# A two-layer DiT on one core: gate sums on VectorE, shorter head norms, a new first-head order and reordered feed-forward openings

## Chip, core and metric

The program runs on 1 core of one Trainium2 chip. The metric is the device time of one execution in microseconds (us). A core has five engines with a queue of instructions each: TensorE (PE in the profile), VectorE (DVE), ScalarE (ACT), GpSimd (POOL) and SyncE (SP, which issues the DMAs).

## What is computed

Two transformer blocks over 512 image tokens and 256 context tokens with D = 1024; only the image rows are returned. Both blocks are modulated by `silu(c) @ ada_w + ada_b` (six chunks: shift, scale and gate for mixer and feed-forward), with one vector for image and one for context tokens. In short:

```
h = concat(image, context)
layer 0:  u = rms_norm(h) * (1 + scale) + shift
          q, k, v = u @ w_qkv;  q, k = rope(rms_norm_per_head(q)), rope(rms_norm_per_head(k))
          h += gate * (softmax(q k^T / 8) v @ w_o)          # 16 heads, 4 key heads of 64
          h += gate_f * swiglu(modulate(rms_norm(h)))       # hidden 2816
layer 1:  HGRN2: q, gate, z_fw, z_bw, v = u @ w_in; f = lb + (1 - lb) sigmoid(z)
          two scans, forward and backward, 8 heads of 128; h += gate * (o @ w_o)
          h += gate_f * swiglu(modulate(rms_norm(h)))
out = rms_norm(h[:512]) * w
```

The large products of float32 matrices are done as three products of fp32r halves.

## The kernel before

Everything lives in SBUF as [128 partitions, tokens], transposed so that channels are partitions. A float32 matrix is held as a high part and a low part: `split` (L86) lets ScalarE cast the high part (`whi`, `hnh`, ...) and VectorE or GpSimd subtract it for the low one (`wlo`, `hnl`, ...). `mm3` (L115 to L118) then issues three matmuls: high x high, high x low, low x high. The order of the instructions on each engine is set by the scheduler of the tile framework, from the program and its own costs; `pin` (keep_in_program_order) holds single instructions in the order written. PSUM has eight banks, given out by name from small pools; a bank comes free when its last reader is done.

The stages, with their places in the trace of before:

- Start (0 to 77 us). The modulation's columns are made in groups on TensorE (`ada_mm`, L185: four matmuls a step, with the two vectors as 32-column weights `cpad`), turned by `ada_put` (L187: a ScalarE copy into `arows`, a transpose into a bank `pta`, an addition on VectorE). `kv_group` (L447) modulates a 128-channel block `xhT[k]` with VectorE, splits it into `hnh` and `hnl`, multiplies it with the key and value weights, and steps the generator `gfill`, which does the remaining groups and then chunk 2, the attention's gate (`ada_chunk(2, ...)`: eight blocks of 128x1024, one step each).
- Query stage (77 to 184). Four weight groups g, each in two parts (`wq`), times three pairs of token tiles: a `q` bank gets 48 products of 128x256. `qk_norm_rope` (L515) squares on ScalarE (L521), sums with VectorE (`ss`, L524), takes the root on ScalarE (L526), does one Newton step with four small VectorE operations (L528 to L531), multiplies (`qhat`, L533; this frees the bank), and turns by the rope tables with VectorE and GpSimd (`qsin`). `k_first` does the same for the keys, casts them twice (`kd`) and transposes them in three `ptk` banks, of which ScalarE and VectorE copy halves to `kT`. `q_first` casts `qd`; GpSimd subtracts its low part; three blocks later eight `ptq` transposes follow. `dfill` does chunk 3 in between, with its sums in `apsum`.
- Attention (184 to 430): `sc` products, softmax on ScalarE and VectorE, `pt` transposes, `po`. Beside it, tiles of the residual are transposed (`rx`) and the gate matrices of chunks 4 and 5 multiplied (`pa`).
- The last part of the output projection with ffn0's opening (430 to 505, `start_attention`), ffn0 (to 977). In ffn openings, operands are block sums and differences of x (`blocks`), made by GpSimd and VectorE, and weights come by `split_next` (weight differences and their split).
- `first_head` (977 to 1003): the first head's three projections, q (image tokens only), z_fw and z_bw, while the last rows of the modulated input (`hn`) still come. Each of two reciprocal roots, image and context, goes: squares added to `acc_n`, `ssq` matmuls, `rc`, a diagonal `dg` on VectorE, `rstd` matmuls.
- Recurrence (1003 to 1436), then `hgrn_wo_last` with ffn1's opening (`start_recurrence`, to 1475): `hwo` products of the last two heads, residual (L687), a square on ScalarE and its addition to `acc_n` on GpSimd (L276), the root for each half of 256 tokens, x by VectorE and ScalarE, cast to `xw`, first `ffi` matmuls. `plain_split` makes the weights' parts.
- ffn1 (to 1813) and the output.

## Time and profile before

| | |
|---|---|
| time, median of 3 runs | 1823.32 us (1820.36 to 1823.44) |
| the profiled execution | 1821.68 us, its span 1819.9 us |
| TensorE busy | 1755.3 us, 96% |
| VectorE busy | 1300.5 us, 71% |
| ScalarE busy | 867.2 us, 48% |
| GpSimd busy | 637.7 us, 35% |
| mean granted TensorE clock | 0.990 |

The profile is one execution. A row of a group gives source line, engine, operation, output and inputs, count and durations. A wait is put down to the instruction whose end came last. The granted clock (PEclk) is 1.00 at full speed and 0.50 when TensorE is throttled. Time in which an engine is idle counts only where TensorE, or the end, waits for it.

### The profile page before, as it was taken

The page shows a single profiled execution, that of the slowest core. Times are in us where ns is not written, and L with a number is a line of the kernel's source. Part 1 is how long each engine was busy: PE and PEld are TensorE (multiplying, and loading weights), DVE is VectorE, ACT ScalarE, POOL GpSimd, SP SyncE. Part 2 cuts the span into 40 slices and gives each one's busy share as a digit, 9 for nine tenths or more (in the row PEclk, how much of TensorE's full clock was granted, in tenths as well). Part 3 has the DMA queues.
Part 4 walks back from the last instruction along what each step waited for, and adds up shares of the span by engine and source line. Part 5 has one row for each costly group of instructions (what it writes and reads, how often), then busy time and mean ns, then how long its engine had stood idle before and what let it go on. Part 6 is the DMA issues. An engine that isn't in the chain of part 4 may idle for free.

```text
span 1819.9 us, 30696 instructions
## 1 busy us (share of the span) xinstructions
PE 1755.3 (96%) x11749; PEld 1606.9 (88%) x11749; DVE 1300.5 (71%) x2291; ACT 867.2 (48%) x1768; POOL 637.7 (35%) x583
## 2 busy tenths in 40 slices
PE   8988999999999999999999999999999899999998
PEld 6778678988899999999998999899898799999997
DVE  4587588888888878787865555665747758786764
ACT  4342787676642424333354443343434445554545
POOL 1244254345522304131414333144325544443420
PEclk9999999999999999999999999999999999999999
DMA  8533520002124243445331211222211223333322
GB/s 319 176 105 84 163 79 24 1 24 64 30 87 129 73 137 93 146 133 153 108 116 34 70 59 59 70 82 70 81 56 38 67 59 112 101 106 106 99 60 83
DMA packets 213459, 166.45 MB, mean 91 GB/s; under 512 B 7952, under 2 KB 190400, under 8 KB 213312
## 3 DMA queue, kind: packets, MB, share of 16 engines
q1 hardware_dynamic: 213024, 163.43, 29.2%
...
## 4 chain that ended last, share of the span: by engine, by line
PE 78%; DVE 9%; POOL 4%; ACT 4%; issue 2%; DMA 2%; SPq 0%; POOLq 0%; DVEq 0%; ACTq 0%
PE ffo L118 5%; PE ffo L116 5%; PE ffo L117 5%; PE x L116 4%; PE x L117 4%; PE x L118 4%; PE pt L714 3%; PE y L118 2%; PE y L116 2%; PE y L117 2%; PE lv L1643 2%; PE hz L116 2%; PE hz L117 2%; PE hz L118 2%; PE sc L656 2%
## 5 line engine op out<-in xcount | busy, mean ns | idle before, releaser
L1650 POOL TENSOR_TENSOR KD<-KD,tot 128x384 f32<-128x384 f32 x96 | 102.6, 1092 | 82.1 <-ACT kc L1633 78.4
L704 POOL TENSOR_SCALAR pf<-pf,st 128x768 f32<-128x768 f32 (+1 forms) x96 | 73.6, 769 | 128.1 <-DVE st L703 91.6
L687 DVE SCALAR_TENSOR_TENSOR hT<-ffo,modc,hT 128x512 f32<-128x512 f32 (+1 forms) x122 | 78.7, 649 | 48.2 <-PE ffo L118 48.2
L118 PE MATMUL ffo<-gh,wlo_w 128*128 128x512 f32 (+1 forms) x304 | 102.9, 339 | 0.0
L117 PE MATMUL ffo<-gl,whi_w 128*128 128x512 f32 (+1 forms) x304 | 102.4, 337 | 0.0
L116 PE MATMUL ffo<-gh,whi_w 128*128 128x512 f32 (+1 forms) x304 | 102.0, 338 | 0.0
L239 DVE SCALAR_TENSOR_TENSOR adacc<-adw,csil,adacc 128x512 f32<-128x512 f32 x98 | 84.5, 871 | 7.5 <-DMA adw<-in_ada_w_dram 7.4
L93 DVE TENSOR_TENSOR ptl<-pt,pth 128x384 fp32r<-128x384 f32 (+1 forms) x160 | 79.9, 524 | 12.4 <-ACT pth L88 11.2
L88 ACT CAST pth<-pt 128x384 fp32r<-128x384 f32 (+1 forms) x160 | 69.9, 461 | 34.3 <-PE pt L714 22.6
L700 DVE TENSOR_REDUCE st<-sc 128x1 f32<-128x768 f32 (+1 forms) x96 | 74.2, 773 | 15.3 <-PE sc L657 12.6
L702 ACT ACTIVATE pf<-sc,st 128x768 f32<-128x768 f32 (+1 forms) x96 | 73.4, 765 | 19.3 <-DVE st L700 18.4
L1650 DVE TENSOR_TENSOR QD<-QD,tot 128x256 f32<-128x256 f32 x96 | 52.0, 582 | 41.2 <-PE lv L1643 41.1
L1633 ACT COPY kc<-KD 128x256 f32<-128x256 f32 x112 | 43.4, 414 | 75.8 <-PE lv L1643 43.8
L714 PE MATMUL pt<-ident,pf 128*128 128x128 f32 x448 | 72.2, 275 | 5.2 <-DVE ptl L93 3.9
L116 PE MATMUL ffo<-gh,foh 128*128 128x512 f32 (+1 forms) x186 | 71.4, 384 | 0.0
L118 PE MATMUL ffo<-gh,fol 128*128 128x512 f32 (+1 forms) x186 | 70.8, 381 | 0.2 <-DVE fol L93 0.2
L117 PE MATMUL ffo<-gl,foh 128*128 128x512 f32 (+1 forms) x186 | 70.9, 381 | 0.0
L1709 POOL TENSOR_SCALAR oss<-oss 128x4 f32<-128x4 f32 (+1 forms) x9 | 4.7, 524 | 181.8 <-DVE oss L1708 181.7
L1643 PE MATMUL lv<-QD,kc 128*128 128x128 f32 x448 | 63.4, 286 | 4.5 <-DVE QD L1650 2.4
L1643 PEld LDWEIGHTS lv<-QD,kc 128*128 128x128 f32 x448 | 58.7, 192 | 8.8 <-ACT kc L1633 3.8
L714 PEld LDWEIGHTS pt<-ident,pf 128*128 128x128 f32 x448 | 51.2, 140 | 14.4 <-issue 6.4
L117 PEld LDWEIGHTS ffo<-gl,whi_w 128*128 128x128 f32 x304 | 57.4, 189 | 6.9
...
## 6 DMA issues: line engine op xcount, KB each, us to landing
...
```

The costliest lines, as they stand in the source:

```text
L93: m = (eng or DVE).tensor_tensor(lo, src, hi.bitcast(F32), op=ALU.subtract)
L116: PE.matmul(ps, ahi, bhi, start=first, stop=False, **kw)
L117: PE.matmul(ps, ahi, blo, start=False, stop=False, **kw)
L118: PE.matmul(ps, alo, bhi, start=False, stop=last, **kw)
L239: pin(DVE.scalar_tensor_tensor(a, raw, cc, a, op0=ALU.mult, op1=ALU.add))
L687: DVE.scalar_tensor_tensor(hT[o][:, a:e], ps, mcol(layer, ch, o, v), hT[o][:, a:e], op0=ALU.mult, op1=ALU.add)
L700: DVE.tensor_reduce(st3[:, 0:1], ps[:, :nk], op=ALU.max, axis=AX.X, negate=True)
L702: ACT.activation(pf, ps[:, :nk], AF.Exp, bias=st3[:, 0:1], accum_out=st3[:, 1:2])
L704: POOL.tensor_scalar(pf, pf, st3[:, 2:3], 1.0, op0=ALU.mult, op1=ALU.mult)
L714: PE.transpose(pt[:, i * P : (i + 1) * P], pf[:, (i0 + i) * P : (i0 + i + 1) * P], ident)
L1643: PE.matmul(ps[:, cs], kc[:, cs], mv, start=True, stop=True)
L1650: eng.tensor_tensor(view, view, f, op=ALU.mult)
```

## The change

The edits, in the order of the program:

1. Chunk 2. `ada_shared` replaces `ada_chunk` there: VectorE multiplies six of the eight blocks by the vectors' columns and adds them up in two tiles `asum`, one for each vector (12 operations of 128x1024). TensorE does the steps of blocks 6 and 7 as before, and one product for each sum with `pick`, a matrix that adds over the partitions. The blocks from k = 4 on are modulated together ahead of it, the last two on ScalarE.
2. `qk_norm_rope` folds mean and epsilon into the root's scale and bias and into one combined Newton step: four VectorE operations follow the sum instead of six. `wk` and `wq` are scaled to match.
3. The keys' two casts and the second copy to `kT` go from VectorE to ScalarE. The last q block is first copied to SBUF by VectorE. Chunk 3's transposes go to the second half of the bank that holds its sums.
4. `first_head`: image tokens of all three projections come first, then the contexts; the context's root one step later; one weight split on VectorE instead of GpSimd; in `fo_out` the context's squares of rows up to 4 are added by VectorE.
5. `start_attention`: two weight steps (`split_next`) stand earlier. `start_recurrence`: the squares go to two sums, even rows on GpSimd and odd rows on VectorE (into `x[7]`); four weight splits move; the second root is taken after them; rows 6 and 7 of the last output projection come together.

The core of the diff:

```diff
-    def ada_put(pa, rows, dst, bias, nch, nk):
+    def ada_put(pa, rows, dst, bias, nch, nk, pt=None):
...
-        pt = bank("pta")
+        pt = bank("pta") if pt is None else pt
...
     def ada_chunk(ch, pa, rows, load):
+        pt = None if pa is None else pa[:, 256:512]
...
-    gfill.add(ada_chunk(2, None, lambda: stp.tile(...), xx_tile))
+    def ada_shared(ch, nsum):
...
+            k = step - 1
+            if k >= nsum:
+                products(raws[k], cpad[:, k], k == nsum, False)
+            for v in range(2 if 0 <= k < nsum else 0):
+                cc = csil[:, v, k : k + 1]
+                if k == 0:
+                    pin(DVE.tensor_scalar(sums[v], raws[k], cc, None, op0=ALU.mult))
+                else:
+                    pin(DVE.scalar_tensor_tensor(sums[v], raws[k], cc, sums[v], op0=ALU.mult, op1=ALU.add))
+            yield
+        for v in range(2):
+            products(sums[v], pick[:, v], False, v == 1)
...
+    def first_modulate(k):
+        for v, a, e in SP2:
+            xs, sc, sh = xhT[k][:, a:e], a_c0[:, k, v : v + 1], mcol(0, 0, k, v)
+            if k < KT - 2:
+                DVE.tensor_scalar(xs, xs, sc, sh, op0=ALU.mult, op1=ALU.add)
+            else:
+                ACT.activation(xs, xs, AF.Identity, bias=sh, scale=sc)
+        split(hn_hi[k], hn_lo[k], xhT[k])
+
+    def last_modulates():
+        for k in range(KT // 2, KT):
+            first_modulate(k)
+        yield from ada_shared(2, ADA_SUMS)
...
-        if sc != 1.0:
-            POOL.tensor_scalar(w, w, sc, 1.0, op0=ALU.mult, op1=ALU.mult)
+        POOL.tensor_scalar(w, w, -0.5 * sc / HD, 1.0, op0=ALU.mult, op1=ALU.mult)
...
-        DVE.tensor_scalar(ss, ss, 1.0 / HD, EPS, op0=ALU.mult, op1=ALU.add)
-        ACT.activation(sr, ss, AF.Sqrt)
+        ACT.activation(sr, ss, AF.Sqrt, bias=epst, scale=1.0 / HD)
         DVE.reciprocal(sr, sr)
         DVE.tensor_tensor(sa, sr, sr, op=ALU.mult)
-        DVE.tensor_tensor(sa, sa, ss, op=ALU.mult)
-        DVE.tensor_scalar(sa, sa, -0.5, 1.5, op0=ALU.mult, op1=ALU.add)
-        DVE.tensor_tensor(ss, sr, sa, op=ALU.mult)
+        DVE.scalar_tensor_tensor(sa, ss, HD * EPS, sa, op0=ALU.add, op1=ALU.mult)
+        DVE.scalar_tensor_tensor(ss, sa, -3.0 * HD, sr, op0=ALU.add, op1=ALU.mult)
...
-            DVE.tensor_copy(kd[:, :, :, i]...
+            ACT.copy(kd[:, :, :, i]...
...
-                    DVE.tensor_copy(dst[HD:P], pg[rows])
+                    ACT.copy(dst[HD:P], pg[rows])
...
+        if g == KVH - 1 and tp == 2:
+            raw = qst.tile([P, 512], F32, tag="kraw", bufs=2, name="qraw")
+            DVE.tensor_copy(raw, ps)
+            ps = raw
...
-                sumsq_add(acc_n[:, a:e], ..., POOL if v else DVE,
+                sumsq_add(acc_n[:, a:e], ..., POOL if v and o > 4 else DVE,
...
-        order = [[(0, 0), (1, 0)], [(1, 1), (2, 0)], [(2, 1)]]
+        order = [[(0, 0), (1, 0)], [(2, 0)], [(1, 1)], [(2, 1)]]
...
-                if n_ == 0 and k in (2, 4):
+                if (n_, k) in ((0, 4), (1, 1)):
                     next(ctx)
...
             for i in range(4):
                 b11, b12, b21, b22 = blocks(i)
                 pin(POOL.tensor_tensor(b12, b22, b12, op=ALU.subtract))
+            split_next()
...
+            split_next()
             plain_hidden(0, 1, *ps0)
...
-            split_next()
-            split_next()
...
-                    sumsq_add(acc_n[:, hs], fp, hT[o][:, hs], o, i == 0, POOL, tag="sw", bufs=2, width=512)
-                    if h == 0 and i == 0:
-                        plain_split(0, 0, "l")
-                    if h == 0 and i == KT - 1:
-                        plain_split(0, 1, "l")
-                    if h == 1 and i == 1:
-                        plain_split(1, 0, "l")
+                    if i % 2:
+                        sumsq_add(halfsums(h)[1], fp, hT[o][:, hs], o, i == 1, DVE, ...)
+                    else:
+                        sumsq_add(halfsums(h)[0], fp, hT[o][:, hs], o, i == 0, POOL, tag="sw", bufs=2, width=512)
+                    if h == 0 and i < 2:
+                        plain_split(0, i, "l")
+                    if h == 1 and i == 0:
+                        plain_split(1, 0, "hl")
...
             plain_split(1, 1, "l")
+            rc[1] = rstd_cols(fp, halfsums(1), H, "rc1")
```

How the queues move at three places. First VectorE at the end of the start. Before, these rows stand there (`wlo_wkv` is the low part of the last key and value weights, `modc` the finished gate columns, `wlo_wq` the first query weights, `vv` the values' low part):

```order
L93 TENSOR_TENSOR hnl_101<-xhT_309,hnh_93 128x768
L93 TENSOR_TENSOR hnl_102<-xhT_318,hnh_94 128x768
L93 TENSOR_TENSOR wlo_wkv_572<-raw_wkv_570,whi_wkv_571 128x1024
L195 TENSOR_TENSOR modc_82<-pta,cols_80 128x16
L93 TENSOR_TENSOR wlo_wq_749<-raw_wq_747,whi_wq_748 128x1024
L93 TENSOR_TENSOR wlo_wq_755<-raw_wq_753,whi_wq_754 128x1024
L93 TENSOR_TENSOR vv<-kv_323,vv 128x8x64
```

After, from the sums' third block on:

```order
L460 SCALAR_TENSOR_TENSOR asum_516<-adw_552,csil,asum_516 128x1024
L460 SCALAR_TENSOR_TENSOR asum_517<-adw_552,csil,asum_517 128x1024
L94 TENSOR_TENSOR wlo_wkv_584<-raw_wkv_582,whi_wkv_583 128x1024
L460 SCALAR_TENSOR_TENSOR asum_516<-adw_578,csil,asum_516 128x1024
L460 SCALAR_TENSOR_TENSOR asum_517<-adw_578,csil,asum_517 128x1024
L460 SCALAR_TENSOR_TENSOR asum_516<-adw_600,csil,asum_516 128x1024
L460 SCALAR_TENSOR_TENSOR asum_517<-adw_600,csil,asum_517 128x1024
L460 SCALAR_TENSOR_TENSOR asum_516<-adw_610,csil,asum_516 128x1024
L460 SCALAR_TENSOR_TENSOR asum_517<-adw_610,csil,asum_517 128x1024
L94 TENSOR_TENSOR vv<-kv_327,vv 128x8x64
L94 TENSOR_TENSOR wlo_wq_752<-raw_wq_750,whi_wq_751 128x1024
L198 TENSOR_TENSOR modc_82<-pta,cols_80 128x16
```

The sums surround the last key weights' low part; the first query weights' low parts now stand behind the values.

Second TensorE at the end of the query stage (`ptq` transposes of queries, `sc` scores, `rx` residual transposes, `pa` the products of chunk 4). Before:

```order
L603 MATMUL ptq<-ident,qd 128x128 x16
L656 MATMUL sc<-kT,qT_705 128x512
L657 MATMUL sc<-kT,qT_705 128x512
L656 MATMUL sc<-kT,qT_705 128x256
L657 MATMUL sc<-kT,qT_705 128x256
L603 MATMUL ptq<-ident,qd 128x128 x8
L682 MATMUL rx_2040<-ident,hT_2004 128x128 x2
L603 MATMUL ptq<-ident,qd 128x128 x8
L682 MATMUL rx_2040<-ident,hT_2004 128x128 x4
L185 MATMUL pa<-adw_2120,cpad 32x256 x4
```

After:

```order
L660 MATMUL ptq<-ident,qd 128x128 x16
L713 MATMUL sc<-kT,qT_707 128x512
L714 MATMUL sc<-kT,qT_707 128x512
L713 MATMUL sc<-kT,qT_707 128x256
L714 MATMUL sc<-kT,qT_707 128x256
L660 MATMUL ptq<-ident,qd 128x128 x8
L739 MATMUL rx_2014<-ident,hT_1978 128x128 x6
L713 MATMUL sc<-kT,qT_707 128x512
L714 MATMUL sc<-kT,qT_707 128x512
L713 MATMUL sc<-kT,qT_707 128x256
L714 MATMUL sc<-kT,qT_707 128x256
L660 MATMUL ptq<-ident,qd 128x128 x8
```

The second group of scores and the whole first residual tile now stand ahead of the last eight query transposes.

Third GpSimd in ffn1's opening (`wlo_w`, `w01l` low parts of weights, `sq` a row's squares, `rc` the root). Before, from the last head's root on:

```order
L93 TENSOR_TENSOR wlo_w<-raw_('w', 0, 0)_14910,whi_w 128x1024
L276 TENSOR_TENSOR acc_n<-acc_n,sq_14932 128x256
L276 TENSOR_TENSOR acc_n<-acc_n,sq_14939 128x256
L276 TENSOR_TENSOR acc_n<-acc_n,sq_14946 128x256
L276 TENSOR_TENSOR acc_n<-acc_n,sq_14953 128x256
L276 TENSOR_TENSOR acc_n<-acc_n,sq_14960 128x256
L276 TENSOR_TENSOR acc_n<-acc_n,sq_14970 128x256
L276 TENSOR_TENSOR acc_n<-acc_n,sq_14980 128x256
L276 TENSOR_TENSOR acc_n<-acc_n,sq_15008 128x256
L291 TENSOR_TENSOR rc<-rc,mhalf 128x2
```

After:

```order
L94 TENSOR_TENSOR wlo_w<-raw_('w', 0, 0)_14884,whi_w 128x1024
L94 TENSOR_TENSOR w01l<-raw_('w', 0, 1)_14886,w01h 128x1024
L280 TENSOR_TENSOR acc_n<-acc_n,sq_14916 128x256
L280 TENSOR_TENSOR acc_n<-acc_n,sq_14930 128x256
L280 TENSOR_TENSOR acc_n<-acc_n,sq_14953 128x256
L298 TENSOR_TENSOR rc<-rc,mhalf 128x2
```

A second weight split stands ahead of the sums, and three sums are left ahead of the root.

More of the change, by code (lines that the diff above doesn't have):

```diff
@@ L112, in load_split, with mm3 @@
         return hi, lo
-    def mm3(ps, ahi, alo, bhi, blo, first, last, onto=False):
+    def mm3(ps, ahi, alo, bhi, blo, first, last, onto=False, hold=False):
         kw = dict(skip_group_check=True) if onto else {}
-        PE.matmul(ps, ahi, bhi, start=first, stop=False, **kw)
+        m = PE.matmul(ps, ahi, bhi, start=first, stop=False, **kw)
+        if hold:
+            pin(m)
         PE.matmul(ps, ahi, blo, start=False, stop=False, **kw)
@@ L423, with products @@
         gfill.add(ada_group(*g_))
-    gfill.add(ada_chunk(2, None, lambda: stp.tile([P, 256], F32, tag="arows", bufs=2, name="arows2"), xx_tile))
+    pick = stp.tile([P, 2, 32], F32, name="pick")
+    POOL.memset(pick, 0.0)
+    for v in range(2):
+        POOL.memset(pick[:, v, v : v + 1], 1.0)
+    def ada_shared(ch, nsum):
+        pa = bank("pa")[:, 0:256]
+        sums = [stp.tile([P, D], F32, name=f"asum{v}") for v in range(2)]
+        def products(m, col, start, stop):
+            m4 = m.rearrange("p (b j n) -> p b j n", b=2, j=4)
+            for j in range(4):
+                PE.matmul(pa[32 * j : 32 * (j + 1)], col, m4[:, :, j], start=start, stop=stop)
+        raws = []
+        for step in range(KT + 1):
+            if step < KT:
+                raws.append(xx_tile(f"adw{ch}{step}"))
+                dma(raws[-1], ada_w[0, step * P : (step + 1) * P, ch * D : (ch + 1) * D])
+            k = step - 1
[8 more added lines that the diff above has]
+            yield
+        for v in range(2):
+            products(sums[v], pick[:, v], False, v == 1)
+        rows = stp.tile([P, 256], F32, tag="arows", bufs=2, name="arows2")
+        ada_put(pa, rows, modc[0][:, ch : ch + 1], ada_bias(0, ch, 1), 1, KT)
+    def first_modulate(k):
[10 more added lines that the diff above has]
+        yield from ada_shared(2, ADA_SUMS)
+    gfill.add(last_modulates())
     gfill.step(4)
@@ L450, in kv_group @@
             k = k0 + j
-            for v, a, e in SP2:
-                DVE.tensor_scalar(xhT[k][:, a:e], xhT[k][:, a:e], a_c0[:, k, v : v + 1], mcol(0, 0, k, v),
-                                  op0=ALU.mult, op1=ALU.add)
-            split(hn_hi[k], hn_lo[k], xhT[k])
+            if k < KT // 2:
+                first_modulate(k)
             for t in range(NT):
@@ L566, in k_first @@
         for i in range(2):
-            DVE.tensor_copy(kd[:, :, :, i].rearrange("p t h d -> p (t h) d"), r.rearrange("p t h d -> p (t h) d"))
+            ACT.copy(kd[:, :, :, i].rearrange("p t h d -> p (t h) d"), r.rearrange("p t h d -> p (t h) d"))
         POOL.tensor_tensor(kl, r, kd[:, :, :, 0].bitcast(F32), op=ALU.subtract)
@@ L971, in plain @@
                 ps[h] = xbank("ffi")[:, 0:H]
-            mm3(ps[h], hi[:, c], lo[:, c], xh[:, k % 4], xl[:, k % 4], first, last)
+            mm3(ps[h], hi[:, c], lo[:, c], xh[:, k % 4], xl[:, k % 4], first, last, hold=first and hold)
         gh, gl = {}, {}
@@ L1065, in fo_out @@
             if p_ == len(parts) - 1:
-                sumsq_add(acc_n[:, a:e], late_pool[0], hT[o][:, a:e], o, o == 0, POOL if v else DVE,
+                sumsq_add(acc_n[:, a:e], late_pool[0], hT[o][:, a:e], o, o == 0, POOL if v and o > 4 else DVE,
                           tag=f"g{8 + (o + v) % 2}", bufs=1, width=n)
```

49 lines of the change are left out of this document (31 added, 18 removed).

## The prediction

> **What bounds the kernel now.** I read the page first, then TensorE's waits, then the granted clock around the longest of them. The page's span, TensorE's busy row and the chain that ended last:
>
> ```profile
> span 1819.9 us, 30696 instructions
> PE 1755.3 (96%) x11749; PEld 1606.9 (88%) x11749; DVE 1300.5 (71%) x2291; ACT 867.2 (48%) x1768; POOL 637.7 (35%) x583
> PE 78%; DVE 9%; POOL 4%; ACT 4%; issue 2%; DMA 2%; SPq 0%; POOLq 0%; DVEq 0%; ACTq 0%
> ```
>
> TensorE works in 96% of the span, and the diff takes only a few matmuls away. So the time can fall almost only by what TensorE waits for. Its waits by releaser (total us, times, longest):
>
> ```profile
> PE q L117 <- DVE wlo_wq L93: 3.7, 2, 2.4
> PE sc L656 <- DVE qhat L533: 3.5, 1, 3.5
> ...
> PE pta L193 <- ACT kT L582: 3.3, 1, 3.3
> PE ssq L282 <- POOL acc_n L276: 3.2, 1, 3.2
> PE rstd L301 <- DVE dg L297: 3.1, 2, 1.6
> ...
> PE y L118 <- DVE wlo_w L93: 2.3, 1, 2.3
> ...
> PE ffi L116 <- ACT xw L88: 1.8, 1, 1.8
> ...
> PE ptk L578 <- ACT qT L606: 1.5, 1, 1.5
> ...
> PE ptk L578 <- DVE kT L588: 0.8, 1, 0.8
> ...
> PE h L116 <- DVE hT L687: 0.7, 1, 0.7
> ```
>
> All ten lie in stages that the diff touches. Four of them are followed by a stretch at half clock (columns of the windows: stretch, length, busy time of PE, PEld, DVE, ACT, POOL, then the granted clock):
>
> ```profile
> 121.20:128.00 6.80, 6.06 (x29) 6.06 (x30) 5.55 (x13) 1.85 (x5) 3.36 (x5) 0.50 0.01 1
> 134.90:138.30 3.40, 2.78 (x23) 2.78 (x24) 3.30 (x7) 0.21 (x1) 1.73 (x1) 1.00 0.47 137
> 179.20:182.60 3.40, 3.40 (x14) 3.21 (x15) 2.68 (x4) 0.64 (x2) 0.00 (x0) 0.50 1.19 289
> 493.20:500.00 6.80, 6.01 (x18) 5.14 (x17) 6.22 (x13) 5.62 (x13) 1.17 (x1) 0.50 0.35 97
> 1449.00:1455.80 6.80, 4.69 (x21) 4.38 (x21) 5.65 (x15) 5.17 (x15) 5.46 (x8) 0.50 0.00 1
> ```
>
> The wait of 3.3 (pta) ends at 121.9, that of 3.5 (sc) at 179.2, that of 2.3 (y) at 491.9, that of 3.2 (ssq) at 1447.3: each stands at or just before a clock of 0.50. After the 2.4 us wait for wlo_wq, which ends at 135.5, the clock stays 1.00. At half clock TensorE does half the work, so the stretches at 121, 179 and 1449 cost at most 3.4, 1.7 and 3.4 us besides the waits.
>
> The profiled execution took 1821.68 us, 1.8 of them outside the span; the median of the runs is 1823.32. I sum against 1821.7.
>
> **1. The start: eight TensorE steps become four.** A step of the gate's chunk and the kv matmuls around it, then VectorE there:
>
> ```profile
> 58.62 0.39 PE L118 MATMUL kv<-whi_wkv,hnl 128*128 128x512 f32 x1
> 58.95 0.64 PE L185 MATMUL pa<-adw,cpad 128*32 128x256 f32 x8
> 59.52 0.50 PE L116 MATMUL kv<-whi_wkv,hnh 128*128 128x512 f32 x1
> 59.85 0.40 PE L117 MATMUL kv<-wlo_wkv,hnh 128*128 128x512 f32 x1
> 60.09 0.39 PE L118 MATMUL kv<-whi_wkv,hnl 128*128 128x512 f32 x1
> ...
> 56.47 1.23 DVE L93 TENSOR_TENSOR wlo_wkv<-raw_wkv,whi_wkv 128x1024 fp32r<-128x1024 f32 x1
> 70.75 0.17 DVE L195 TENSOR_TENSOR modc<-pta,cols 128x16 f32<-128x16 f32 x1 [13.06 <-PE pta L193]
> ```
>
> Undisturbed kv matmuls start 0.24 apart (59.85 to 60.09); from 58.62 to 59.85 there are two of them and a step, so a step costs 1.23 - 0.47 = 0.76, and four fewer save 3.0 us. VectorE gets 12 operations of 128x1024, by the row at 56.47 some 1.2 each: 14 us into the 13.06 it stood idle. But in the new order ScalarE modulates blocks 6 and 7 and casts hnh for 4 to 6 ahead of the weights' high part for k = 4, and VectorE does six sums before wlo_wkv of k = 6. TensorE, 3 us early at k = 4, then waits about 1.5 and 0.5 us for these. SyncE's issues of the rope tables and of raw_wq stand behind the last two blocks of the sums and move from about 54 to about 60; they are first used after 77. I take a gain of 1.0 (from -2.5, if the sums delay the first key chain, to +1.5).
>
> **2. The query stage: VectorE gets shorter, a bank goes.** The groups of the norm, of the keys' casts and copies (count: min/median/max ns):
>
> ```profile
> L525 DVE TENSOR_SCALAR ss<-ss x15: 164/570/792, 76.0 to 176.3; 128x8 f32<-128x8 f32 x15
> L567 DVE CAST kd<-qrot x6: 416/418/427, 82.4 to 113.8; 128x512 fp32r<-128x512 f32 x6
> L588 DVE CAST kT<-ptk x6: 684/690/695, 95.5 to 129.2; 64x512 fp32r<-64x512 f32 x6
> ```
>
> Two operations less per call save 15 x (0.57 + 0.16) = 11; kd and kT go to ScalarE and save 6 x 0.42 + 6 x 0.69 = 6.6: together 17.7 us of VectorE. TensorE loses 12.7 us there: 3.7 + 3.3 + 1.5 + 0.8 by the waits, 3.4 by the clock. The chunk's transposes now go to the bank of their own sums, whose copy was long done: the pta wait and its half clock, 6.7 us, go whole. The other 6.0 I do not count whole: TensorE will run 6.7 us ahead of before, and VectorE must follow; ScalarE now makes both copies of a key bank one after the other. I count 1.3 of them: 8.0 in all (4 if the waits at key banks stay, 11 if nearly everything goes).
>
> The L525 operation takes 0.57 at the median and 0.16 alone. One of them, and what ran on GpSimd:
>
> ```profile
> 175.73 1.26 POOL L597 TENSOR_TENSOR qd<-qrot,qd 128x512 fp32r<-128x512 f32 x1 [1.33 <-DVE qd L596]
> 176.28 0.74 DVE L525 TENSOR_SCALAR ss<-ss 128x8 f32<-128x8 f32 x1
> ```
>
> It ends at 177.02, when GpSimd's qd ends (176.99). The Trainium skill, page "SBUF — State Buffer", section "Who interferes with whom", says that VectorE operations with two SBUF inputs, too, are locked out while a GpSimd operation reads SBUF. By that rule part of the stall would move to the next product of `ss` rather than go: about 0.4 of the 0.74 a call, and the 11 us of saving would be nearer 7, still enough to cover the 6.0.
>
> **3. The end of the stage.** The sc wait ends at 179.2 with the last qhat, the norm's product, which frees the q bank. Now VectorE copies that bank to SBUF ahead of the norm: it has cast the block before at 175.7 (GpSimd's qd starts then), and a copy of that size (0.69, as kT) ends at 176.4, while TensorE has 16 transposes to do. What comes behind on ScalarE, from the rows of before:
>
> ```profile
> 184.37 0.81 ACT L683 COPY hT<-rx 128x768 f32<-128x768 f32 x1
> 185.19 1.28 ACT L702 ACT_TABLE_LOAD   x1
> 186.49 0.90 ACT L702 ACTIVATE pf<-sc,st 128x768 f32<-128x768 f32 x1
> ```
>
> Wait and half clock, 3.5 + 1.7, go but for 0.3. New in the list: the second sc waits for ScalarE's copy of the first residual tile (0.8), the next residual for the first softmax (1.28 + 0.90, less some 0.5 of TensorE's own work: 1.7). Gain 5.2 - 0.3 - 0.8 - 1.7 = 2.4 (0 if the new waits reach the old, 4.5 if they are hidden).
>
> **4. ffn0's opening.** GpSimd's sums stand ahead of the two weight splits on VectorE's side of the list; but VectorE still has a dozen operations before the split that y waits for (2.3 us). Gain 0 (-2 to +3); the cover is gone if GpSimd's four sums alternate with VectorE's.
>
> **5. The first head.** VectorE's diagonal and what GpSimd did:
>
> ```profile
> 970.19 1.53 POOL L276 TENSOR_TENSOR acc_n<-acc_n,sq 128x256 f32<-128x256 f32 x2
> 971.76 0.69 DVE L297 TENSOR_TENSOR dg<-ident,rc 128x512 f32<-128x512 f32 x1 [2.38 <-POOL acc_n L276]
> ```
>
> One weight split and the context's first sums move from GpSimd to VectorE, so dg no longer waits for acc_n (its buffer): the first rstd wait of 1.6 shrinks to about 0.65, the second, 1.5, goes since the root comes a step later, h's 0.7 loses 0.2. The context step follows sooner, though, and may wait 0.3 for its rows. 0.95 + 1.5 + 0.2 - 0.3 = 2.3 (0 to 3.5).
>
> **6. ffn1's opening.** GpSimd before, and the casts that ScalarE moves ahead:
>
> ```profile
> 1435.05 2.39 POOL L93 TENSOR_TENSOR wlo_w<-raw_('w', 0, 0)_14910,whi_w 128x1024 fp32r<-128x1024 f32 x1
> 1439.67 8.21 POOL L276 TENSOR_TENSOR acc_n<-acc_n,sq 128x256 f32<-128x256 f32 x8 [2.23 <-ACT sq L275]
> 1460.14 1.04 ACT L88 CAST whi_w<-raw_('w', 2, 1)_15109 128x1024 fp32r<-128x1024 f32 x1
> ```
>
> TensorE's wait there, in its own row:
>
> ```profile
> 1447.26 0.61 PE L282 MATMUL ssq<-ones,acc_n 128*128 128x2 f32 x4 [3.23 <-POOL acc_n L276]
> ```
>
> Lost here: 3.2 (ssq) + 3.4 (clock) + 1.8 (ffi) = 8.4. After: GpSimd does two splits of 2.39 from 1435.05 on, some half a microsecond between them for the second's high part, to about 1440.3, then three sums instead of eight, the last behind two of VectorE's, to about 1443.5. TensorE came to ssq at 1447.26 - 3.23 = 1444.0; ssq now stands 18 half-width matmuls of 0.12 sooner, at 1441.8: it waits 1.7. ScalarE casts both halves of slice 2 (1.04 each, the second only when hwo's weights are free) before the first row of x: TensorE waits some 2.4 at ffi. With 0.3 for four more ssq matmuls 4.4 stay: gain 4.0 (0 if either new wait brings half clock again, 7 if GpSimd is not held up).
>
> **Nothing** for the pinned first ffi matmul, the scaled `wk` (one small GpSimd operation, long before use) and the root's scale and bias, which ride in an instruction that is there already.
>
> **Sum:** 1.0 + 8.0 + 2.4 + 0 + 2.3 + 4.0 = 17.7; 1821.7 - 17.7 = 1804.0 us.
>
> **Rivals.** (a) *The half clock stays.* Even if the waits go, the stretches at 0.50 may come wherever a new wait of about 2 us stands (parts 3 and 6): 3.4 + 1.7 + 3.4 = 8.5 more, 1812.5. For it: y's wait of only 2.3 was followed by one. Against: the wait at 121.9 has no successor in the new list. The Trainium skill, page "TensorE: Matmul & The Clock Gate", section "HAM oscillation — how this bites in real kernels", gives idle gaps above about 3.4 us as the limit; by that the gaps of 3.2 and 3.3 would not be the cause, and this rival is what follows. Here the clock of 0.50 after them speaks against it. Chance 0.12.
>
> (b) *The key banks wait for ScalarE.* The pta wait ended with a ScalarE copy of kT; if the next transposes wait for ScalarE's doubled copies instead, part 2 gives nothing: 1812.0. Against: ScalarE is busy under half of the stage. Chance 0.14.
>
> (c) *Slower: the sums.* If each of the 12 sums is held up by one GpSimd operation (2.39 as at 1435), VectorE ends 28.7 us later, and TensorE, in order, stands before the products; with 2 us of slack 26.7 more, 1830.7. It turns the sign from (17.7 + 2) / 12 = 1.6 us per sum. Against it GpSimd's work there:
>
> ```profile
> 48.00:75.00 27.00, 27.00 (x157) 17.52 (x156) 12.22 (x20) 8.86 (x12) 3.96 (x11) 1.00 0.57 200
> ```
>
> Eleven operations and 3.96 us in all. Chance 0.05.
>
> (d) *The waits are only replaced by others of their length*: 1821.7. Chance 0.05.
>
> **How the numbers follow.** The forecast has 0.64. The parts' ends, taken as independent (root of the squares), give 7.7 above and 5.7 below 1804.0; (a) and (b) lie just outside, so the range goes to 1815, and down to 1797. A measurement of this kernel tells about 0.2%, 3.6 us, from no change. Faster: 0.64 + 0.12 + 0.14 = 0.90; same: (d), 0.05; slower: (c), 0.05.
>
> **What would show it.** Right: no wait at the chunk's transposes and no half clock near 121, 179 and 1449; sc's wait under 1 us; ssq's near 1.7; ffi's first near 2.4; the first q matmul about 1 us before 77.1. Wrong: TensorE waiting at the products of the sums or at wlo_wkv for more than 2 us; VectorE's 128x1024 sums above 1.6; waits on kT of more than 3 us; half clock in the ffn1 opening.

## The result, and the profile after

The changed kernel takes 1813.51 us (median of 6 runs, 1809.85 to 1814.73), the kernel before 1822.62 (6 runs, 1820.24 to 1823.44): a ratio of 0.995, 95% interval 0.9939 to 0.9962, or 9.1 us less. Beside later experiments, on another chip, it was 1814.40 against 1819.84: 0.9971 (0.9959 to 0.9984), 5.4 us less. The change is faster, since both intervals lie below 1, by a third to a half of the forecast 17.7 us.

The page after: TensorE works in 97% of the span.

```profile
span 1810.8 us, 30614 instructions
PE 1752.7 (97%) x11725; PEld 1607.7 (89%) x11725; DVE 1308.5 (72%) x2267; ACT 875.3 (48%) x1784; POOL 637.4 (35%) x576
```

VectorE is busier, not less (1300.5 before): its 12 sums of 128x1024 outweigh what the norm and the keys save. TensorE's waits after, by releaser (total us, times, longest), those that answer to the list of the prediction:

```profile
PE y L121 <- DVE wlo_w L94: 3.4, 1, 3.4
...
PE ptk L631 <- ACT qT L663: 2.5, 1, 2.5
...
PE ffi L120 <- DVE xw L94: 2.3, 1, 2.3
PE ffi L117 <- ACT xw L89: 2.2, 1, 2.2
...
PE ssq L288 <- POOL acc_n L280: 2.0, 1, 2.0
...
PE q L120 <- DVE wlo_wq L94: 1.2, 1, 1.2
PE rstd L308 <- DVE dg L304: 1.2, 1, 1.2
...
PE sc L713 <- ACT hT L740: 0.9, 1, 0.9
PE rx L739 <- ACT pf L759: 0.9, 1, 0.9
```

The waits at chunk 3's transposes (`pta`, 3.3) and for the last `qhat` (`sc`, 3.5) are gone. The row for `ffi` from VectorE's `xw` is new; no term of the prediction had it. The stretches at half clock after, from 99 to 1455 us (stretch, length, busy time of PE, PEld, DVE, ACT, POOL, then the granted clock):

```profile
99.70:106.50 6.80, 6.09 (x35) 4.50 (x36) 5.37 (x13) 4.18 (x10) 2.17 (x5) 0.50 0.61 173
482.00:488.80 6.80, 6.15 (x19) 5.33 (x18) 5.99 (x12) 5.08 (x12) 0.25 (x1) 0.50 0.26 77
775.50:778.90 3.40, 3.40 (x16) 3.40 (x15) 2.97 (x6) 1.14 (x2) 0.00 (x0) 0.51 0.64 207
1393.40:1396.80 3.40, 3.40 (x17) 3.22 (x16) 3.40 (x10) 0.89 (x2) 0.45 (x1) 0.51 0.23 68
1441.10:1444.50 3.40, 3.40 (x18) 3.40 (x18) 2.45 (x7) 3.40 (x11) 1.84 (x3) 0.51 0.00 0
1451.40:1454.80 3.40, 3.40 (x18) 3.40 (x18) 0.49 (x2) 0.38 (x1) 0.00 (x0) 0.50 0.51 151
```

The one near 179 is gone; the one at 121 is gone, but one at 99.7 came; ffn1's opening has two, of 3.4 each, instead of one of 6.8.

Where the time went, from the starts of TensorE's own rows (the second profile of the change is that of the later measurement):

| part: from, to | forecast gain | before, us | after, us | after, second profile |
|---|---|---|---|---|
| 1: start to the first `q` matmul | 1.0 | 77.1 | 74.8 | 75.8 |
| 2: to the last `q` matmul | 8.0 | 96.5 | 91.3 | 91.4 |
| 3: to the last `po` matmul | 2.4 | 252.9 | 249.6 | 249.5 |
| 4: first `z` to first `w` of ffn0 | 0 | 13.3 | 13.7 | 13.0 |
| 5: first `ffo` to last `h` | 2.3 | 467.6 | 465.4 | 464.0 |
| 6: last pair of `ho` to the last `rstd` group | 4.0 | 30.4 | 33.2 | 33.2 |

The two rows of part 6, of before and of after:

```profile
1432.18 0.39 PE L1700 MATMUL ho<-S,QD 128*128 128x128 f32 x2
...
1462.60 0.61 PE L301 MATMUL rstd<-c,ones 128*128 128x128 f32 x4
```

```profile
1419.98 0.39 PE L1767 MATMUL ho<-S,QD 128*128 128x128 f32 x2
...
1453.22 1.05 PE L308 MATMUL rstd<-c,ones 128*128 128x128 f32 x4
```

Part 6 was to gain 4.0 and loses 2.8: this one stage is 6.8 of the missing 8.6 us (17.7 forecast, 9.1 measured). Part 2 lacks 2.8 and part 4 0.4; parts 1 and 3 bring 2.2 more than forecast in the first profile.

### The profile page after: what moved, and what is told of

Its sections match the earlier page's. It is cut to its first block, busy times and chain, and to the rows that moved or that the text cites. A ratio compares the mean times of both kernels' runs of the same rounds, so it can differ in the third digit from the quotient of the medians.

```text
span 1810.8 us, 30614 instructions
## 1 busy us (share of the span) xinstructions
PE 1752.7 (97%) x11725; PEld 1607.7 (89%) x11725; DVE 1308.5 (72%) x2267; ACT 875.3 (48%) x1784; POOL 637.4 (35%) x576
## 4 chain that ended last, share of the span: by engine, by line
PE 79%; DVE 8%; issue 4%; ACT 4%; POOL 4%; DMA 1%; POOLq 0%; SPq 0%; DVEq 0%; ACTq 0%
PE ffo L121 5%; PE ffo L117 5%; PE ffo L120 5%; PE x L117 4%; PE x L120 4%; PE x L121 4%; PE lv L1710 3%; PE pt L771 3%; PE y L121 2%; PE y L117 2%; PE y L120 2%; PE hz L117 2%; PE hz L120 2%; PE hz L121 2%; PE sc L713 1%
## 5 line engine op out<-in xcount | busy, mean ns | idle before, releaser
L1717 POOL TENSOR_TENSOR KD<-KD,tot 128x384 f32<-128x384 f32 x96 | 102.5, 1091 | 81.8 <-ACT kc L1700 78.0
L120 PE MATMUL ffo<-gl,whi_w 128*128 128x512 f32 (+1 forms) x304 | 102.5, 337 | 0.0
L757 DVE TENSOR_REDUCE st<-sc 128x1 f32<-128x768 f32 (+1 forms) x96 | 74.0, 772 | 10.4 <-PE sc L714 9.0
L771 PEld LDWEIGHTS pt<-ident,pf 128*128 128x128 f32 x448 | 51.2, 140 | 13.8 <-issue 6.2
```

Of the source, the lines that this page charges most:

```text
L120: PE.matmul(ps, ahi, blo, start=False, stop=False, **kw)
L757: DVE.tensor_reduce(st3[:, 0:1], ps[:, :nk], op=ALU.max, axis=AX.X, negate=True)
L771: PE.transpose(pt[:, i * P : (i + 1) * P], pf[:, (i0 + i) * P : (i0 + i + 1) * P], ident)
L1717: eng.tensor_tensor(view, view, f, op=ALU.mult)
```

## Why part 6 loses: GpSimd's new split

VectorE and GpSimd of after, where TensorE waits for `xw`, each in its own timeline:

```profile
1443.14 0.41 DVE L94 TENSOR_TENSOR xw<-x,xw 128x256 fp32r<-128x256 f32 x1
...
1447.67 2.56 DVE L94 TENSOR_TENSOR xw<-x,xw 128x256 fp32r<-128x256 f32 x1
```

```profile
1447.42 2.53 POOL L94 TENSOR_TENSOR w11l<-raw_('w', 1, 1)_14890,w11h 128x1024 fp32r<-128x1024 f32 x1
```

and TensorE:

```profile
1450.29 0.38 PE L120 MATMUL ffi<-xw,whi_w 128*128 128x256 f32 x1 [2.27 <-DVE xw L94]
```

One line of the whole diff, not among those printed above, chooses the engine of these splits:

```diff
-            pool_ = (j, i) == (0, 0) or j > 1 and i if layer else j == 0
+            pool_ = j == 0 or i if layer else j == 0
```

The new rule gives the low part of weight (1, 1) to GpSimd, too. GpSimd's split starts 0.25 us ahead of VectorE's low part of x, and that operation, 0.41 us a little earlier, takes 2.56: it ends at 1450.23, 0.28 after GpSimd's. TensorE stands for 2.27. This is the rule that the prediction cited for the norm's products (the Trainium skill, page "SBUF — State Buffer", section "Who interferes with whom": a VectorE instruction with two inputs in SBUF is blocked, not slowed, while a GpSimd instruction reads SBUF). The trace agrees, and the price is larger here: 2.15 us on the one operation, where the prediction took about 0.4 for a call of the norm. The prediction's working had counted GpSimd's two splits of weight 0 and overlooked this third one.

Four kernels tested it. The kernel before took 1821.8 us beside experiments 1, 2, 3 and 8, 1821.24 beside 4 to 7, and 1819.84 beside 9 to 12; a ratio is to that time, with its 95% interval.

**Experiment 1: that split back on VectorE.**

```diff
-            pool_ = j == 0 or i if layer else j == 0
+            pool_ = j == 0 or j > 1 and i if layer else j == 0
```

> The changed kernel with one split, w11l of slice 1's second part, back on VectorE; nothing else moves. Theory A (GpSimd's split of 2.53 us locks VectorE's low part of x out, 2.56 us for an operation of 0.41, and so makes TensorE's wait of 2.27 at ffi and the half clock behind it): the wait falls below 0.5 us, the time from 1813.5 to between 1809.5 and 1811.5. Rival B (VectorE is late anyway, since the second root stands ahead of that low part, and now has 1.2 us more to do): the wait stays above 1.5 us and the time within 1 us of 1813.5.

Measured: 1812.13 us, ratio 0.9947 (0.9931 to 0.9963), not to be told from the change itself, and outside both theories' ranges of time. Its first `q` matmul came 2.6 us later in the profiled run, with a DMA wait of 2.2 that ended at 34.6 us in the start, so the stage must be read by itself. There the `ffi` wait for `xw` is gone, and so is the second half clock. VectorE's rows at that place:

```profile
1450.36 0.75 DVE L94 TENSOR_TENSOR xw<-x,xw 128x256 fp32r<-128x256 f32 x2
1451.03 1.21 DVE L94 TENSOR_TENSOR w11l<-raw_('w', 1, 1)_14890,w11h 128x1024 fp32r<-128x1024 f32 x1
```

Two operations on x in 0.75, then the split in 1.21, half of what it takes on GpSimd. From `ho` to `rstd` it is 30.6 us (33.2 with the change): 2.6 back, so the wait is theory A's, and with the half clock behind it it makes 2.6 of the 6.8 that the stage lacks.

**Experiment 2: the whole of part 6 undone**, all else as changed.

> The changed kernel without the whole edit of ffn1's opening (start_recurrence, rows 6 and 7 of the last output projection, the split rule and the held matmul as before). Theory A (the edit of ffn1's opening costs about 2 us in all, since a new wait and two half-clock stretches replace what it saves): 1810 to 1812.5, so faster than the changed kernel. Rival B (it saves the 4 us forecast, and the shortfall lies elsewhere): 1816.5 to 1818.5. Rival C (neither gain nor loss): 1812.5 to 1814.5.

Measured: 1810.61 us, 0.9945 (0.9931 to 0.9959); the stage takes 31.4 us, with the old wait of 3.2 at `ssq` and a half clock of 10.2 us. So part 6 as it was made costs 1.9 us in its stage (33.24 against 31.37), though the changed kernel had less half clock there, 6.8 us.

**Experiment 3: the split back, and ScalarE's casts of slice 2 after x.** The prediction had put TensorE's wait at the first `ffi` down to those two casts of 1.04. ScalarE in after, ahead of the first row of x:

```profile
1436.32 1.05 ACT L89 CAST whi_w<-raw_('w', 2, 0)_15074 128x1024 fp32r<-128x1024 f32 x1 [1.18 <-PE hwo L120]
...
1437.79 1.03 ACT L89 CAST whi_w<-raw_('w', 2, 1)_15076 128x1024 fp32r<-128x1024 f32 x1
1438.72 0.51 ACT L1019 ACTIVATE x<-x,modc 128x256 f32<-128x256 f32 x1
```

```diff
+            pool_ = j == 0 or j > 1 and i if layer else j == 0
...
-            plain_split(2, 0, "l")
+            plain_split(2, 0, "hl")
-            plain_split(2, 1, "l")
+            plain_split(2, 1, "hl")
```

> As e1_split_back, and the two casts of slice 2's high weights on ScalarE held behind the first rows of x. Theory A: TensorE's wait at the first ffi falls from 2.24 to about 1.2 us, and the lock-out wait goes: 1808 to 1810.5. Rival B (the first ffi waits for the root and the chain behind it, not for the casts): its wait stays above 2 us and the time is that of e1_split_back.

Measured: 1808.82 us, 0.994 (0.9923 to 0.9956). The first `ffi` wait is 1.5 (2.2), so the two casts make 0.8 of it (2.24 to 1.48) and not the whole; in what is left ScalarE itself waits 1.07 for VectorE's first row of x. The stage is 29.3 us: 3.9 under the change, 1.1 under before, and still 2.9 above the 26.4 that the forecast makes it (30.4 - 4.0). It has 3.4 us at half clock.

**Experiment 4: part 6 alone on the kernel before.**

> Kernel: the kernel before with the change's part at ffn1's opening alone. Theory A (as it was made, this part costs: GpSimd's second split holds VectorE's low part of x, and TensorE waits at the first products): slower by 1 to 3 us, 1823 to 1825 against 1821.8. The recorded forecast: 4.0 us faster, 1817.8. If half clocks decide it by chance: anywhere between, with a half clock between 1440 and 1456 in the profile or without.

Measured: 1826.40 us, 1.0038 (1.0025 to 1.005): slower, by 5.2 us, theory A's sign and more than its 1 to 3. The stage takes 35.9 us (30.4). Its waits there:

```profile
PE ssq L286 <- POOL acc_n L278: 3.0, 1, 3.0
PE ffi L116 <- ACT xw L88: 2.5, 1, 2.5
PE ffi L119 <- DVE xw L93: 2.3, 1, 2.3
```

The wait for `xw` is there to the tenth, so it belongs to part 6 and to nothing else in the change. That the part costs 5.5 us in its stage here, and 1.9 by experiment 2, lies only in part in the clock. This profile has 10.2 us at half clock in the stage, the changed kernel's 6.8; the opening as it was before has 6.8 in the kernel before (30.4 us) and 10.2 in experiments 2, 5 and 6 (31.4, 31.5, 31.1 us). At equal half clock the part costs 2.8 (33.2 against 30.4, with 6.8) and 4.5 to 4.9 (35.9 against these three, with 10.2). The first two waits here are 1.2 us longer in sum than in the changed kernel; the rest of the difference stays open. That the part costs time is shown; how much depends on what stands around it.

## Why part 2 gives 5.2: the end of VectorE's chain sets the stage

The prediction valued the query stage by TensorE's waits: 6.7 us for chunk 3's transposes and the half clock behind them, and 1.3 of the rest. The first edit can be made alone.

**Experiment 5: only the bank of chunk 3's transposes**, on the kernel before.

```diff
+        pt = None if pa is None else pa[:, 256:512]
...
+        pt = bank("pta") if pt is None else pt
```

> Kernel: the kernel before with one edit, the chunk's transposes in the bank of its own sums. It removes the wait of 3.3 us for ScalarE's kT and the half clock behind it, 6.7 us together by the recorded working. Theory A (VectorE's chain to wlo_wq sets the stage, and what TensorE gains ahead of it is handed back at the next wait for wlo_wq, which grows): 0 to 2 us faster, 1819.8 to 1821.8, with a wait for wlo_wq above 4 us. Theory B (the wait and its half clock are the loss, as the prediction counted): 6.7 us faster, 1815.1, waits for wlo_wq unchanged at 3.7.

Measured: 1822.01 us, 1.0004 (0.9995 to 1.0013): nothing. The 3.3 us are gone from its list of waits, and come back at `wlo_wq` (two waits of 2.4 and 1.3 before, one of 5.1 now) and at `whi_wq` (new); the wait for `qhat` stands as before:

```profile
PE q L117 <- DVE wlo_wq L93: 5.1, 1, 5.1
PE sc L657 <- DVE qhat L534: 3.5, 1, 3.5
PE q L116 <- ACT whi_wq L88: 1.6, 1, 1.6
```

What stands in the way is the low part of the third weight group's second half. The matmul that waits for it, with its wait, of before, of this kernel, and of the change:

```profile
135.52 0.39 PE L117 MATMUL q<-wlo_wq,hnh 128*128 128x256 f32 x1 [2.42 <-DVE wlo_wq L93]
```

```profile
134.77 0.58 PE L117 MATMUL q<-wlo_wq,hnh 128*128 128x256 f32 x1 [5.14 <-DVE wlo_wq L93]
```

```profile
129.59 0.39 PE L120 MATMUL q<-wlo_wq,hnh 128*128 128x256 f32 x1 [1.21 <-DVE wlo_wq L94]
```

Counted from each profile's first `q` matmul (77.08, 76.43, 74.77), it is released after 58.4, 58.3 and 54.8 us, whatever TensorE had lost on the way: if TensorE is early, it waits longer. Experiment 4 shows the same with its query stage left as it was before: there the `pta` wait was 1.85 and no half clock followed it, the wait for `wlo_wq` was 5.14, and the release came after 58.5 us (135.14 less 76.68). The weight arrives when VectorE's list says so. So only what shortens that list counts, and the change took 3.6 us out of it. The other 1.6 of the 5.2 lie behind the release (38.1 us to the last `q` matmul before, 36.5 after), where a second wait for `wlo_wq`, 1.3 at 156.6 us, is gone. The list of after, up to the split:

```profile
119.07 1.32 DVE L596 TENSOR_TENSOR qrot<-qhat,cwq 128x256 f32<-128x256 f32 x2
121.17 0.69 DVE L605 TENSOR_TENSOR qrot<-qrot,qsin 128x512 f32<-128x512 f32 x1 [0.78 <-POOL qsin L601]
...
123.36 0.20 DVE L581 RECIPROCAL ss<-ss 128x8 f32<-128x8 f32 x1 [0.29 <-ACT ss L580]
...
127.25 0.69 DVE L605 TENSOR_TENSOR qrot<-qrot,qsin 128x512 f32<-128x512 f32 x1 [1.20 <-POOL qsin L601]
...
128.32 1.22 DVE L94 TENSOR_TENSOR wlo_wq<-raw_wq,whi_wq 128x1024 fp32r<-128x1024 f32 x1
```

VectorE waits in it for GpSimd's `qsin` and ScalarE's root. The 17.7 us of VectorE's work that the prediction counted as saved (by chance the same number as its whole forecast) could not turn into as much time: it is saved over the whole stage, partly behind the release, and the list is a chain over three engines, in order on each. Little of the saving moved on to the products of `ss` behind it. In the third of the 15 calls the second product now stands while GpSimd reads, 1.30 instead of 0.17 (VectorE, then GpSimd):

```profile
90.84 1.30 DVE L583 SCALAR_TENSOR_TENSOR ss<-ss 128x8 f32<-128x8 f32 x1
```

```profile
90.81 1.31 POOL L654 TENSOR_TENSOR qd<-qrot,qd 128x512 fp32r<-128x512 f32 x1 [1.26 <-DVE ss L582]
```

It ends at 92.14, GpSimd's `qd` at 92.12, as the Trainium skill's rule in the section named above has it; but before the change the first product of the same call had taken 1.26. The other 14 calls have this product at 0.17. Over the stage the norm's products and scalings took 19.5 us before and 9.9 after: 9.6 of the 11 us counted were saved, not the 7 that the prediction expected by that rule (its 15 calls of 0.4 would even have left 5).

**Experiment 6: the query stage's part alone** (parts 2 and 3) on the kernel before.

> Kernel: the kernel before with the query stage's part of the change alone (the chunk's transposes in the bank of its sums, the shorter norm, the keys' casts and second copies on ScalarE, the copy of the last q bank ahead of its norm). Theory A (what the trace after shows: the stage itself gains 5.2 us, because the weights' low part stands at the end of a chain on VectorE that did not get shorter by as much as TensorE got earlier; the end of the stage gains 3.3): 8.5 us faster than before, about 1813.3 against 1821.8, with a wait for wlo_wq between 1 and 4 us left. The recorded forecast (8.0 + 2.4 = 10.4): 1811.4, with that wait gone. Theory C (the gain of the stage is given back later, by other phases of the clock): under 6 us, above 1815.8.

Measured: 1812.34 us, 0.9954 (0.9942 to 0.9965): 8.9 less, theory A's 8.5. The interval, 6.4 to 10.6 us, does not quite exclude the forecast's 10.4; the trace does: the query stage takes 91.1 us, and a wait of 3.5 for `wlo_wq` is left. This part alone brings as much as the whole change (9.1 and 5.4), so the other parts come to little in sum.

**Experiment 7: a shorter norm.** On the kernel of experiment 3, the correction step is left out of the norm, as its expectation says.

```diff
-        DVE.tensor_tensor(sa, sr, sr, op=ALU.mult)
-        DVE.scalar_tensor_tensor(sa, ss, HD * EPS, sa, op0=ALU.add, op1=ALU.mult)
-        DVE.scalar_tensor_tensor(ss, sa, -3.0 * HD, sr, op0=ALU.add, op1=ALU.mult)
```

> Kernel: the fastest one so far (the change with GpSimd's extra split back on VectorE and ScalarE's casts of slice 2 behind the first rows of x, 1808.8 us), in which the norm of the query stage leaves out the correction step, three operations of 128x8 on VectorE per call, 45 in all (a part of the computation that is left out; a scalar of the norm's weights is set to suit). Theory A (VectorE's chain to wlo_wq sets the query stage's length): three operations of 0.17 to 0.2, and up to 1.3 where one is held up by GpSimd, go from each of six calls ahead of the wait: the wait for wlo_wq of 2.5 shrinks to under 1, the stage from 92.2 to 89 or 90, the time is 2 to 3 us less, about 1806. Theory B (the stage is set by TensorE and ScalarE, and the wait for wlo_wq is only where it shows): no change, 1808.8, the stage stays within 0.5 of 92.

Measured: 1805.68 us, 0.9929 (0.9912 to 0.9945), 3.1 under the kernel of experiment 3 by the medians of two chips, 2 by the ratios, whose intervals overlap. The stage shows it better. Waits of its query stage:

```profile
PE ptk L628 <- ACT qT L660: 2.2, 1, 2.2
...
PE q L120 <- DVE wlo_wq L94: 0.6, 1, 0.6
```

The stage takes 87.3 us (92.2); 1.5 of the 4.9 are a half clock behind `wlo_wq` that did not come here, as experiment 9 shows. TensorE's instructions are the same, and the release came after 50.7 us instead of 54.1: VectorE's chain sets the stage.

**Experiment 8: the keys' casts back on VectorE.** The changed kernel waits 2.5 us at `ptk`, where ScalarE now casts `kd` ahead of `qT`. This undoes it:

```diff
-            ACT.copy(kd[:, :, :, i].rearrange("p t h d -> p (t h) d"), r.rearrange("p t h d -> p (t h) d"))
+            DVE.tensor_copy(kd[:, :, :, i].rearrange("p t h d -> p (t h) d"), r.rearrange("p t h d -> p (t h) d"))
```

> The changed kernel with the two casts of each key block (kd) back on VectorE. Theory A (ScalarE is late with the query's transposed copies because kd's casts, a square and two weight casts stand before them; so TensorE waits 0.75 and 2.52 us at the key transposes and falls to half clock at 99.7): the two waits together fall from 3.3 to below 2 us and the time by 1.5 to 5 us, to between 1808.5 and 1812. Rival B (the wait comes from the weight casts and VectorE loses what ScalarE gains): waits move to wlo_wq, time 1812.5 to 1815.

Measured: 1812.66 us, 0.9952 (0.994 to 0.9965), no difference. The theory of that run (the `ptk` wait is what part 2 lacks) fell: the waits there became 2.3 and 3.1 instead of 0.75 and 2.5, and the stage took 92.0 us instead of 91.3. The time lost at `ptk` is mostly paid back at the wait for `wlo_wq`, 0.9.

**Experiment 9: the weight's buffer free earlier**, on the kernel of experiment 3.

```diff
-                ks = list(range(KT)) if tt == 0 else list(range(4, KT)) + list(range(4))
+                ks = list(range(KT)) if tt == 0 or tp == 2 else list(range(4, KT)) + list(range(4))
```

> Kernel: the fastest complete one so far, with TensorE alone changed: in the last block of each group of query weights the second half runs over the weight tiles in rising order, so that the first tile's buffer comes free 1.6 us sooner for the next group's. VectorE's and ScalarE's instructions and their order stay. Theory A (the low part of the weights stands behind VectorE's norm chain, not behind its buffer): the split ends when it did, the stage stays at 92.2 within 0.4, time 1808.8. Theory B (the buffer's release sets it): the wait for wlo_wq of 2.5 shrinks by 1 to 1.6, the stage and the time with it, 1807.4.

Measured: 1808.79 us, 0.9938 (0.9925 to 0.9952), the time of experiment 3. The waiting matmuls of experiment 3 and of this one:

```profile
129.28 0.39 PE L120 MATMUL q<-wlo_wq,hnh 128*128 128x256 f32 x1 [2.55 <-DVE wlo_wq L94]
```

```profile
129.01 0.39 PE L120 MATMUL q<-wlo_wq,hnh 128*128 128x256 f32 x1 [2.38 <-DVE wlo_wq L94]
```

Both are 54.14 us behind their first `q` matmul (75.14 and 74.87): the buffer does not set it. The stage is 1.6 shorter in this profile (90.6 against 92.2) where the clock differs: no half clock followed the wait here, 3.4 us of it did in experiment 3. That this is the clock's and not the edit's, the other profiles with the shorter norm show: from the release to the last `q` matmul it is 36.5 us in all five without a half clock there (the change twice, experiments 1, 8 and 9) and 37.9 to 38.0 in all five with 3.4 us of it (experiments 2, 3, 6, 10 and 12).

**Experiment 10: four casts of query blocks on ScalarE**, to shorten VectorE's list, on the kernel of experiment 12 below.

```diff
-        DVE.tensor_copy(qd[:, :, :, g % 2], r)
+        (ACT.copy if g < 2 and tp < 2 else DVE.tensor_copy)(qd[:, :, :, g % 2], r)
```

> Kernel: the one before last but two (both weight splits of ffn0 back), and ScalarE instead of VectorE casts the query blocks of the first two groups to their high part (four casts of 0.43 off VectorE, about 0.6 each on ScalarE); one of the two splits that stood ahead of the sixth block's norm moves behind it. Theory A (VectorE's chain to wlo_wq sets the stage): the split that TensorE waits for comes about 0.4 us sooner and the second one no longer stands in the norm's way; the stage is 0.4 to 1.5 us shorter, the time about 1807.5. Rival (ScalarE's part of the chain grows by as much: its cast is 0.2 longer and stands behind the copies of kT): no gain, or up to 1 us slower, 1808.3 to 1809.3.

Measured: 1812.63 us, 0.9965 (0.9953 to 0.9978): slower by 4.8 us than the same without it, where theory A had expected 0.4 faster and the rival up to 1 slower. ScalarE in this kernel:

```profile
123.85 0.62 ACT L653 CAST qd<-qrot 128x512 fp32r<-128x512 f32 x1 [4.35 <-DVE qrot L605]
124.38 0.59 ACT L575 ACTIVATE qrot<-q 128x512 f32<-128x512 f32 x1
124.87 1.07 ACT L635 CAST kT<-ptk 128x512 fp32r<-128x512 f32 x2
...
128.20 0.30 ACT L580 ACTIVATE ss<-ss,epst 128x8 f32<-128x8 f32 x1
```

The cast waits 4.35 us for VectorE, and behind it in ScalarE's queue stand the next block's square, four copies of keys, and the root for which VectorE then waits 2.76. Counted from the first `q` matmul the square starts at 47.8 us; in the kernel of experiment 12 (118.34) it was 42.7. The release came after 57.6 us instead of 54.8, and the stage took 95.7 instead of 92.8. The 0.43 us saved for each cast were nothing against a wait put at the head of another queue. The stage accounts for 2.9 of the 4.8 us; 1.0 lies in the start of this profile, for which the edit gives no reason.

## The half clock, and part 4

**Experiment 11: the change again.**

> Kernel: the change itself, again, beside the three others on one chip, so that the fastest variant is compared with it directly. Expected 1812.8 (the mean of its two medians of ratio, 0.995 of 1821.9), against 1808 to 1809 for the two variants: 4 us apart. In its profile the waits stand where they stood (ssq 2.0, x's low part 2.3, ptk 2.5); if half-clock stretches come by the phase of a free-running window, they stand at other waits or with other lengths than in the first profile, at the same waits' lengths.

Measured: the 0.9971 given above. Its waits in the changed stages are those of the first profile within 0.2 us, but for 2.4 instead of 1.2 at `wlo_wq`. The clock at three of the stretches that the first profile has at half clock (the first behind `ptk`, then at 775 and at 1393):

```profile
102.50:105.90 3.40, 3.40 (x25) 2.06 (x24) 2.08 (x6) 1.88 (x4) 2.14 (x4) 0.50 0.82 240
...
775.00:779.00 4.00, 3.18 (x29) 3.19 (x30) 3.58 (x8) 1.14 (x2) 0.00 (x0) 1.00 0.43 117
1392.00:1397.00 5.00, 3.96 (x27) 3.47 (x28) 5.00 (x12) 1.94 (x5) 1.24 (x3) 1.00 0.34 99
```

The waits of 2.5 at 775 and of 1.57 at 1393 brought no half clock here; in the first profile 2.4 and 1.58 did. So whether a stretch at half clock follows a wait of this length differs between executions of one kernel, and the execution's time with it. The Trainium skill, page "TensorE: Matmul & The Clock Gate", section "What's actually happening", has a free-running window of 3413 ns behind the gate; here the lengths are 3.4, 6.8 and 10.2. Its limit for gaps, about 3.4 us (the section that the prediction cites), is too wide for this kernel: a stretch followed the wait of 1.58, with no other wait above 0.52 in the 9 us ahead of it.

**Experiment 12: ffn0's two weight splits back as before**, on the kernel of experiment 3.

```diff
-            split_next()
             for i in range(4):
                 b11, b12, b21, b22 = blocks(i)
                 pin(DVE.scalar_tensor_tensor(b22, b11, -1.0, b22, op0=ALU.mult, op1=ALU.subtract))
-            split_next()
...
+            split_next()
+            split_next()
             xops["t3"] = operand("t3")
```

> Kernel: the fastest complete one so far (the change with GpSimd's extra split back on VectorE and ScalarE's casts of slice 2 behind the first rows of x), and the two weight splits of ffn0's opening back behind GpSimd's and VectorE's differences as before the change. Theory A (the earlier splits cost: TensorE waits 3.4 us at y instead of 2.3, while the stretch that follows is not shorter): the wait at y is 2.3 again, the time from z's first matmul to w's first is 0.4 to 0.6 us shorter than 13.0, the time about 0.5 us less, 1808.3. Forecast's theory (nothing there): 1808.8 with the same stretch of 13.0. A median here can hardly tell 0.5 us; the trace's stretch is to decide.

Measured: 1807.88 us, 0.9938 (0.9926 to 0.995). The stage from `z` to `w` is 12.4 us, against 13.0 in experiment 3:

```profile
477.41 0.33 PE L117 MATMUL z<-xb21h,whi_w 128*128 128x384 f32 x1
...
489.82 0.44 PE L117 MATMUL w<-xt4h,whi_w 128*128 128x384 f32 x1 [0.62 <-ACT xt4h L89]
```

Without these edits it is 12.4 to 12.7 in five profiles and 13.3 in the one before, with them 13.0 to 13.8 in eight. So part 4 costs about 0.6 by the traces, too little for the medians to tell. This kernel had no half clock at the wait of 2.3 there, and experiment 4, with the same wait and 6.8 us of half clock, took 12.4 us as well: TensorE's speed does not set that stage there, and the stretch at half clock was free. It was so wherever it began 4.5 to 5.8 us behind `z`; in the three profiles where it began 6.7 to 7.1 behind (before, the change, experiment 1) the stage is 0.6 to 0.9 longer than in the others of its kind. Against the change itself on the same chip it is the faster complete kernel, 0.9938 (0.9926 to 0.995) to 0.9971 (0.9959 to 0.9984): 6.5 us by the medians.

## Why the prediction was right in direction and wrong in size

- **The sum**: 1804.0 us was 9.5 too low, and about half of the forecast gain came. That the time lies in the range is luck: the parts' own ends reached to 1811.7, and the range was carried on to 1815 for rivals (a) and (b). Rival (b) did not come, and (a) at most in ffn1's opening.
- **Part 6 was the failed step**: "GpSimd does two splits of 2.39 from 1435.05 on". There are three; the third held VectorE's low part of x for 2.56 us instead of 0.41, and TensorE waited 2.27 (experiments 1 and 4). The sum's two other terms came as forecast: `ssq` waits 2.0 (forecast 1.7), the first `ffi` 2.2 (2.4). The second failed term is the half clock, of which 3.4 us were counted as gained: the opening has 6.8 us at 0.50 before and after. After, 3.4 of them follow the first `ffi` wait, which the sum had forecast at 2.4 without a half clock, and 3.4 follow the wait for `xw`. The gain of 4.0 became a loss of 2.8: waits of 6.5 instead of 5.0, and 0.3 for more `ssq` matmuls, make 1.8 of it; 1.0 stays open. The prediction had named the condition on which its gain falls to 0, half clock behind a new wait, but not the third wait, which makes it a loss.
- **Part 2, mechanism wrong in one term, right in another.** "the pta wait and its half clock, 6.7 us, go whole": the wait went, the time did not (experiment 5), because the release of `wlo_wq`, 58.4 us behind the first `q` matmul, stayed where it was. What did gain, 5.2 with a forecast of 8.0, was VectorE's shorter list, which the prediction had counted only as a cover; that the two numbers are near is luck. Rival (b) named a wait for ScalarE at the key banks; the 2.5 at `ptk` is one, but it is not what bounds (experiment 8).
- **Half clock** as a price: half of each stretch's length was charged. Ahead of `wlo_wq` it is absorbed (6.8 us of it at 99.7 and 3.4 at 102.5 in the two profiles of the change, none in experiment 12, and the release comes after 54.8 or 54.9 us in all three), at ffn0 it cost nothing or up to 0.9, and behind `wlo_wq` it cost 1.5 of 3.4. Rival (a), that stretches come at any new wait of about 2 us, was true of the stretches (99.7, 1441, 1451); of their price it was not true at 99.7, and in ffn1's opening the price was not measured by itself.
- **Part 3** gained 3.3 (2.4): the new waits for ScalarE are 0.9 and 0.9, not 0.8 and 1.7.
- **Part 1** gained 2.3 and 1.3 in two profiles (1.0), but the first `q` matmul comes at 76.4 to 77.7 in the four profiles with the old start and at 74.6 to 77.4 in the ten with the new, so single profiles do not tell 1 from 2. TensorE's waits for the weights' parts there were 1.0 and 0.3 instead of 1.5 and 0.5. Rival (c), that GpSimd holds up the sums, did not come (none took more than 1.28). **Part 5** gained 2.2 and 3.6 (2.3), the second without the half clock at 775. **Part 4**: 0 was forecast, the cost is about 0.6.
